# A hybrid encoder block: its 45 inverse square roots move from VectorE to one GpSimd power instruction each

## The chip, the cores and the metric

The kernel runs on one core of a Trainium2 chip. The metric is the device time of one execution in microseconds (us). The engines are named as the profile names them: PE is TensorE (matmuls and transposes), DVE is VectorE, ACT is ScalarE, POOL is GpSimd, SP is SyncE, which issues most DMAs.

## The reference

One encoder block on 1024 tokens of width 1024, all in float32:

```python
h = rmsnorm(x, norm1_w); p = h @ w_in
# branch A: differential attention, 8 heads, with rmsnorm over each head's 128 output channels
# branch B: gated DeltaNet, 8 heads, forward and backward scans
qg, kg = l2norm(qg), l2norm(kg)
og = rmsnorm(o_fwd + o_bwd, gdn_norm_w) * silu(z)
merged = sigmoid(gate_a) * (oa @ w_proj_attn) + sigmoid(gate_g) * (og @ w_proj_gdn)
x = x + merged @ w_out
x = x + expert_choice_ffn(rmsnorm(x, norm2_w), ...)   # 16 experts, 128 tokens each
out = rmsnorm(x, norm_f_w)
def rmsnorm(t, w): return t * lax.rsqrt(mean(t * t) + 1e-6) * w
```

Every `rsqrt` above is what this case is about: one number per token (first norm, router norm, final norm), or per token and head (l2norm of keys and queries, the ends of DeltaNet heads and of attention heads).

## The kernel before

The work is done in stages that overlap: the first norm of 8 tiles of 128 tokens; 8 DeltaNet heads; 8 attention heads; the two branch projections, the output projection and the router; and 16 experts in 64 units. Exact float32 products are made of three fp32r matmuls: each weight is split into a high part (ACT, `cp`) and a low part (a subtraction, on POOL by `ptt` for the dense weights `W`, on DVE for the experts).

**The order is planned.** Every engine call goes through `Emit.op` (line 273) with a planned cost in ns; a greedy list scheduler (`run`, line 356) takes, among all tasks, the operation that can start first by its own clocks of the five engines and a table of latencies between engines (line 52), and writes it into that engine's stream. So the streams are fixed when the program is built, each engine runs its own in order, and a changed cost or a changed engine moves much of what follows, also of what the edit does not name. `e.cp` is ACT's copy, `e.ts`, `e.tt` and `e.stt` are DVE's scalar, two-operand and fused steps, `e.ptt` and `e.pts` are POOL's.

**The root.** `rsqrt` (line 528) computes y = x^(-1/2) on DVE by an integer estimate (two `ts`) and three Newton steps of three instructions, 11 in a chain. `prsqrt` (line 516) does the estimate on DVE and the three Newton steps, of four instructions each, on POOL. The callers are:

- `norm_tile` (line 719): 8 tiles, one column; the result scales the tile on DVE (even tiles) or ACT and POOL (odd ones), then PE transposes it.
- `Head.main` (line 946): 8 heads, 16 columns (keys and queries); `irk`, `rk2`, `bp` and `nbp` follow on DVE.
- `Head.finish` (line 1159): 8 heads, 8 columns; the result times `aq` scales the head's output `oa` on DVE (line 1175, recorded at L409), which PE then transposes.
- `Attn.finish` (line 1368): 8 heads, 8 columns, in the same way.
- `router` (line 1555): `prsqrt` for 7 tiles, `rsqrt` for the last.
- `final_pair` (line 1939): 4 pairs of final row tiles, two columns; and `Experts.last` (line 1877): the last expert's rows.

In the profile, helpers carry the line: L409 is `tt`, L428 and L429 are `ts`, L434 is `stt`, L413 is `ptt`, L403 is `act`, L391 a matmul, L395 a transpose.

Of the kernel before, what the change touches and what calls it, by code (L numbers as in the profile page):

```python
# [108 lines left out]
class Emit:  # L109
# [403 lines left out]
                lambda: (self.nc.gpsimd.tensor_scalar(out, a, s1, None, op0=op0) if s2 is None else  # L513
                         self.nc.gpsimd.tensor_scalar(out, a, s1, s2, op0=op0, op1=op1)), [out], [a], 0, "pts")

    def prsqrt(self, y, x, t):

        i = t[:, 1].bitcast(I32)
        t = t[:, 0]
        self.ts(i, x.bitcast(I32), 1, op0=ALU.arith_shift_right)  # L520
        self.ts(y.bitcast(I32), i, -1.0, float(0x5F3759DF), op0=ALU.mult, op1=ALU.add)
        for _ in range(3):
            self.ptt(t, y, y, ALU.mult)
            self.ptt(t, t, x, ALU.mult)
            self.pts(t, t, -0.5, 1.5)
            self.ptt(y, t, y, ALU.mult)

    def rsqrt(self, y, x, t):

        i = t[:, 1].bitcast(I32)  # L530
        t = t[:, 0]
        self.ts(i, x.bitcast(I32), 1, op0=ALU.arith_shift_right)
        self.ts(y.bitcast(I32), i, -1.0, float(0x5F3759DF), op0=ALU.mult, op1=ALU.add)
        for _ in range(3):
            self.tt(t, y, y, ALU.mult)
            self.stt(t, t, -0.5, x, ALU.mult, ALU.mult)
            self.stt(y, t, 1.5, y, ALU.add, ALU.mult)


class Ctx:  # L540
# [178 lines left out]
def norm_tile(g, st, w1):  # L719
    e = g.e  # L720
    xs = yield from e.new("xs", [P, D])
    e.dma(xs.v, g.ins["x"][st * P:(st + 1) * P, :])
    yield
    ss, rs = g.nsm[:, st:st + 1], g.nsm[:, 8 + st:9 + st]
    e.act(g.jk.v, xs.v, AF.Square, accum_out=ss)
    e.ts(ss, ss, 1.0 / D, 1e-6)
    e.rsqrt(rs, ss, g.nsm[:, 16 + 2 * st:18 + 2 * st].rearrange("p (a b) -> p a b", b=1))
    yield
    if st % 2:
        e.cp(xs.v, xs.v, scale=rs)  # L730
        e.ptt(xs.v, xs.v, w1.v, ALU.mult)
    else:
        e.stt(xs.v, xs.v, rs, w1.v, ALU.mult, ALU.mult)
    pt = yield from e.new("n0", [P, 8, P])
    for d in range(8):
        e.tr(pt[:, d, :], xs[:, d * P:(d + 1) * P], g.ident.v)
    yield
    o = slice(st * P, (st + 1) * P)
    e.cp(g.hh[:, :, o], pt.v)
    e.tt(g.hl[:, :, o], pt.v, f32(g.hh[:, :, o]), ALU.subtract)  # L740
    e.free(xs, pt)

    def done():
        g.tiles.add(st)
        g.hready[0] = g.tiles >= {0, 1, 2, 3}
        g.hready[1] = len(g.tiles) == 8
    e.then(done)
    if st == 7:
        e.free(w1, g.jk)
        e.close("xs", "w1", "n0", "jk")  # L750


def norm_first(g):
    e = g.e
    g.hT = e.now_new("hh", [P, 8, S], F32R), e.now_new("hl", [P, 8, S], F32R)
    g.hh, g.hl = g.hT[0].v, g.hT[1].v
    g.nsm = e.now_new("nsm", [P, 96]).v
    g.hready, g.tiles = [False, False], set()
    w1 = e.now_new("w1", [P, D])
    g.jk = e.now_new("jk", [P, D])  # L760
    e.spawn(norm_tile(g, 0, w1), 0)
    yield
    e.dma(w1.v, bcast(g.ins["norm1_w"], [P, D]))
    e.dma(g.ident.v, g.ins["c_ident"])
    for st in range(1, NT):
        e.spawn(norm_tile(g, st, w1), 0)
        yield
# [96 lines left out]
class Head:  # L864
# [81 lines left out]
    def main(self):  # L946
# [24 lines left out]
                e.free(pt)  # L971
                yield
        e.ts(ss, ss, 1e-6, op0=ALU.add)
        e.rsqrt(rk, ss, rt)
        e.tt(irk, rk[:, 0:8], ss[:, 0:8], ALU.mult)
        e.tt(rk2, rk[:, 0:8], rk[:, 0:8], ALU.mult)
        if not g.logits:
# [181 lines left out]
    def finish(self):  # L1159
# [10 lines left out]
        e.tt(m2, aq, aq, ALU.mult)  # L1170
        e.tt(m2, m2, sq, ALU.mult)
        e.ts(m2, m2, 1.0 / 128, 1e-6)
        e.rsqrt(rr, m2, rt)
        e.tt(rr, rr, aq, ALU.mult)
        e.tt(oa.v, oa.v, bcast(rr[:, :, None], [P, NT, P]), ALU.mult)
        yield
# [48 lines left out]
class Attn:  # L1225
# [142 lines left out]
    def finish(self):  # L1368
        g, e, o, sm = self.g, self.g.e, self.o, self.sm
        ss, rr = sm[:, 0:8], sm[:, 8:16]  # L1370
        e.ts(ss, ss, 1.0 / 128, 1e-6)
        e.rsqrt(rr, ss, sm[:, 16:32].rearrange("p (a b) -> p a b", b=8))
        e.tt(o.v, o.v, bcast(rr[:, :, None], [P, NT, P]), ALU.mult)
        yield
        for half in range(2):
# [179 lines left out]
def router(g, st, xt, po):  # L1555
# [21 lines left out]
        e.free(pt)  # L1577
        yield
    e.ts(ss, ss, 1.0 / D, 1e-6)
    (e.rsqrt if st == NT - 1 else e.prsqrt)(rs, ss, sm[:, 4:6].rearrange("p (a b) -> p a b", b=1))  # L1580
    pl = yield from e.new("gp", [P, 512])
    for d in range(8):
        e.mm(pl[:, 0:16], hT[:, d, :], g.wr[:, d, :], d == 0, d == 7)
# [150 lines left out]
class Experts:  # L1734
# [142 lines left out]
    def last(self, pd):  # L1877

        g, e, x, fs = self.g, self.g.e, self.xl, self.fs
        for c in range(2):  # L1880
            cs = slice(c * 512, c * 512 + 512)
            e.stt(x[:, cs], pd[:, cs], g.hval[:, NE - 1:NE], x[:, cs], ALU.mult, ALU.add)
        ss, rs, rt = fs[:, 64:65], fs[:, 65:66], fs[:, 66:68]
        e.act(pd.v, x.v, AF.Square, accum_out=ss)
        e.ts(ss, ss, 1.0 / D, 1e-6)
        e.rsqrt(rs, ss, rt.rearrange("p (a b) -> p a b", b=1))
        e.stt(x.v, x.v, rs, g.wf.v, ALU.mult, ALU.mult)
        if g.finished < NT:
            yield lambda: g.finished == NT
        e.scatter(g.out, g.tok[:, NE - 1:NE], x.v)  # L1890
# [48 lines left out]
def final_pair(g, st, xs, fs):  # L1939
# [4 lines left out]
        e.act(jk.v, x.v, AF.Square, accum_out=ss[:, i:i + 1])  # L1944
        e.free(jk)
    e.ts(ss, ss, 1.0 / D, 1e-6)
    e.rsqrt(rs, ss, fs[:, 16 + 2 * st:20 + 2 * st].rearrange("p (a b) -> p a b", b=2))
    for i, x in enumerate(xs):
        if i and st < 6:
            e.cp(x.v, x.v, scale=rs[:, 1:2])  # L1950
# [32 lines left out]
def body(tc, ins, out, dbg=None, heads=H):  # L1983
# [3 lines left out]
    with ExitStack() as ctx:  # L1987
# [16 lines left out]
        g.hval = e.now_new("hval", [P, 16])  # L2004
        g.tok = e.now_new("tok", [P, 16], I32)
        g.one = e.now_new("one", [P, 64])
        g.logits = g.gdn_done = g.gdn_close = g.attn_ok = g.routes = g.route0 = g.list1 = g.rank_ok = False
        g.ranked = g.h2_rows = 0
        g.attn_done = g.lanes = g.wo = g.routed = g.scattered = 0
# [148 lines left out]
```

## Time and profile before

| | |
|---|---|
| three runs | 3036.37 to 3043.48 us, median 3042.06 |
| the profiled execution | 3041.05 us |
| its span (first to last instruction) | 3039.3 us |
| granted TensorE clock, mean | 0.981 of full speed |
| PE / DVE / ACT / POOL busy | 95% / 78% / 58% / 19% |
| chain that ended last | PE 70%, DVE 15%, ACT 3%, DMA 3%, POOL 1% |

Read the busy shares first, then the table by stage: a saving on an engine counts only in a stage where some other engine waits for it. The chain that ended last is followed back from the end of the program, at each step to what released it. Times in the rows are us from the start of the span.

### The profile page before, as it was taken

How to read it: one execution, taken by the hardware profiler on the slowest of the kernel's cores; microseconds unless marked ns; L12 is line 12 of the kernel's file. 1: busy time of each engine (PE TensorE's matmuls, PEld its weight loads, DVE VectorE, ACT ScalarE, POOL GpSimd, SP SyncE). 2: the span in 40 equal slices, each digit the busy share in tenths (PEclk: the TensorE clock that was granted, in tenths of full speed). 3: DMA queues.
4: the chain of work that ended last, by engine and by line, in shares of the span. 5: the costliest groups of instructions: out<-in, count | busy, mean ns of one | idle time of the engine just before them, and what ended most of it. 6: DMA issues, size and time to landing. Idle time of an engine off the chain costs nothing.

```text
span 3039.3 us, 40711 instructions
## 1 busy us (share of the span) xinstructions
PE 2874.6 (95%) x14780; PEld 2401.8 (79%) x14780; DVE 2371.7 (78%) x3948; ACT 1752.0 (58%) x2668; POOL 567.5 (19%) x448
## 2 busy tenths in 40 slices
PE   7999999899998999999999997899999999999996
PEld 6787887788787878888888786788888888888884
DVE  7768778777865777777862458899888989989887
ACT  5435445444534666776662323577767777777775
POOL 3222222222212211211216332500000000000001
PEclk9999999999999999999999997899999999999998
DMA  4222322321322111112459736899999999999995
GB/s 139 52 68 83 84 61 60 90 63 52 89 74 61 49 49 49 49 49 56 112 161 290 231 105 246 311 390 378 372 386 381 380 383 377 378 377 381 373 355 235
DMA packets 203642, 598.75 MB, mean 197 GB/s; under 512 B 84384, under 2 KB 102304, under 8 KB 154288
## 3 DMA queue, kind: packets, MB, share of 16 engines
q1 hardware_dynamic: 189856, 562.06, 51.4%
q0 software_dynamic: 13584, 34.08, 4.0%
q8 instruction: 116, 1.90, 0.3%
q14 instruction: 86, 0.70, 0.1%
HBM read 535.19 MB, written 52.49 MB: 193 GB/s over the span
## 4 chain that ended last, share of the span: by engine, by line
PE 70%; DVE 15%; ACT 3%; DMA 3%; issue 3%; SPq 1%; POOL 1%; POOLq 0%; DVEq 0%; ACTq 0%
PE psum L391 66%; DVE B L409 6%; PE psum L395 4%; DVE B L434 4%; ACT B L403 2%; DVE B L451 2%; SPq L483 1%; ACT psum L403 1%; DMA dw<-B 1%; DVE B L428 1%; DVE B L455 0%; POOL W L413 0%; ACT W L403 0%; DMA A<-dh,C 0%; DMA B<-dl 0%
## 5 line engine op out<-in xcount | busy, mean ns | idle before, releaser
L391 PE MATMUL psum<-A,W 128*128 128x512 f32 (+1 forms) x5856 | 1548.6, 404 | 13.8 <-POOL W L413 5.5
L391 PEld LDWEIGHTS psum<-A,W 128*128 128x128 f32 (+1 forms) x5856 | 1068.0, 189 | 213.4 <-DVE A L409 10.2
L391 PE MATMUL psum<-B 128*128 128x128 f32 (+3 forms) x3494 | 651.6, 324 | 15.9 <-DVE B L455 7.6
L391 PEld LDWEIGHTS psum<-B 128*128 128x128 f32 x3494 | 544.8, 191 | 92.4 <-DVE B L455 11.1
L403 ACT ACTIVATE B<-psum 128x512 f32<-128x512 f32 (+4 forms) x612 | 266.4, 441 | 400.4 <-PE psum L395 225.3
L403 ACT ACTIVATE B<-B 128x2048 fp32r<-128x2048 f32 (+4 forms) x341 | 381.8, 1130 | 183.3 <-DVE B L434 80.8
L413 POOL TENSOR_TENSOR W<-W,W 128x1024 fp32r<-128x1024 f32 (+1 forms) x105 | 265.2, 2527 | 945.9 <-ACT W L403 818.1
L409 DVE TENSOR_TENSOR B<-B,B 128x2048 fp32r<-128x2048 f32 (+2 forms) x189 | 377.3, 2006 | 34.0 <-ACT B L403 27.1
L391 PE MATMUL psum<-B,W 128*128 128x512 f32 x1536 | 374.0, 395 | 4.0 <-DVE B L409 3.8
L391 PEld LDWEIGHTS psum<-B,W 128*128 128x128 f32 x1536 | 286.0, 189 | 74.2 <-DVE B L409 14.8
L403 ACT ACTIVATE B<-psum,B 128x128 f32<-128x128 f32 (+2 forms) x264 | 190.9, 728 | 197.4 <-PE psum L391 124.7
L395 PE MATMUL psum<-C,B 128*128 128x128 f32 (+1 forms) x1392 | 218.9, 281 | 71.7 <-DVE B L434 28.3
L409 DVE TENSOR_TENSOR A<-B,A 128x2048 fp32r<-128x2048 f32 x112 | 256.7, 2306 | 15.6 <-ACT A L403 14.5
L391 PE MATMUL psum<-A,B 128*128 128x512 f32 x1024 | 264.5, 398 | 2.3 <-DVE A L409 2.3
L395 PEld LDWEIGHTS psum<-C,B 128*128 128x128 f32 (+1 forms) x1392 | 170.6, 144 | 120.7 <-DVE B L434 35.0
L403 ACT ACTIVATE A<-B 128x2048 fp32r<-128x2048 f32 (+1 forms) x121 | 222.7, 1857 | 41.4 <-PE psum L391 20.6
L391 PE MATMUL psum<-B,B 128*128 128x128 f32 (+1 forms) x1024 | 212.6, 294 | 13.7 <-DVE B L460 11.5
L391 PEld LDWEIGHTS psum<-A,B 128*128 128x128 f32 x1024 | 191.0, 189 | 40.5 <-DVE A L409 3.0
L391 PEld LDWEIGHTS psum<-B,B 128*128 128x128 f32 x1024 | 175.4, 192 | 40.9 <-DVE B L460 14.8
L497 POOL DMA_INDIRECT dx<-B,C x15 | 24.3, 1618 | 953.9 <-ACT B L403 953.9
L451 DVE TENSOR_REDUCE B<-psum 128x1 f32<-128x1024 f32 (+1 forms) x136 | 157.3, 1158 | 53.9 <-PE psum L391 53.0
L413 POOL TENSOR_TENSOR B<-B,B 128x128 f32<-128x128 f32 (+3 forms) x98 | 131.6, 1346 | 308.6 <-ACT B L403 218.8
(116 smaller groups left out, 2852.6 us busy)
## 6 DMA issues: line engine op xcount, KB each, us to landing
B<-in_w_gu_dram SPq DMA_DIRECT2D x154, 1024.0 KB, 7.3
A<-in_w_gu_dram SPq DMA_DIRECT2D x77, 1024.0 KB, 7.3
B<-in_w_dn_dram SPq DMA_DIRECT2D x74, 1024.0 KB, 7.3
A<-in_w_dn_dram SPq DMA_DIRECT2D x40, 1024.0 KB, 7.6
W<-in_w_gu_dram SPq DMA_DIRECT2D x25, 1024.0 KB, 7.1
W<-in_w_gdn_dram SPq DMA_DIRECT2D x32, 512.0 KB, 3.7
B<-dG SPq DMA_DIRECT2D x32, 512.0 KB, 5.6
W<-in_w_proj_dram SPq DMA_DIRECT2D x32, 512.0 KB, 4.6
```

Of the source, the lines that this page charges most:

```text
L391: self.op("pe", c, lambda: self.nc.tensor.matmul(out, lhsT, rhs, start=start, stop=stop), [out], [lhsT, rhs], l, "mm")
L395: self.op("pe", 109, lambda: self.nc.tensor.transpose(out, in_, ident), [out], [in_, ident], 55, "tr")
L403: self.op("act", c, lambda: self.nc.scalar.activation(out, in_, func, **kw), [out] + w, [in_] + r, 0, "act")
L409: self.op("dve", 69 + 1.041 * free(out), lambda: self.nc.vector.tensor_tensor(out, a, b, op), [out], [a, b], 0, "tt")
L413: self.op("pool", 150 + 2.104 * free(out), lambda: self.nc.gpsimd.tensor_tensor(out, a, b, op), [out], [a, b], 0, "ptt")
L428: lambda: (self.nc.vector.tensor_scalar(out, a, s1, None, op0=op0) if s2 is None else self.nc.vector.tensor_scalar(out, a, s1, s2, op0=op0 ...
L434: lambda: self.nc.vector.scalar_tensor_tensor(out, a, s, b, op0=op0, op1=op1),
L451: self.op("dve", 69 + 1.041 * free(in_), lambda: self.nc.vector.tensor_reduce(out, in_, axis=AX.X, op=op), [out], [in_], 0, "red")
L483: self.op("sp", 478, lambda: self.nc.sync.dma_start(out, in_), [out], [in_], 0, "dma", max(n / 360.0, 112))
L497: self.op("pool", 1100, lambda: self.nc.gpsimd.indirect_dma_start(out=dst, out_offset=bass.IndirectOffsetOnAxis(ap=idx, axis=0), in_=y, in ...
```

## The change

`rsqrt` becomes one instruction on POOL: a two-operand instruction with the operation `pow`, whose second operand is a column that holds -0.5, broadcast along the row (`e.half`, column 63 of the tile `one`, set once by a memset on POOL). `prsqrt` and the scratch columns go. The planner is told a cost of 150 + 20 n ns for n columns.

```diff
-    def prsqrt(self, y, x, t):
-
-        i = t[:, 1].bitcast(I32)
-        t = t[:, 0]
-        self.ts(i, x.bitcast(I32), 1, op0=ALU.arith_shift_right)
-        self.ts(y.bitcast(I32), i, -1.0, float(0x5F3759DF), op0=ALU.mult, op1=ALU.add)
-        for _ in range(3):
-            self.ptt(t, y, y, ALU.mult)
-            self.ptt(t, t, x, ALU.mult)
-            self.pts(t, t, -0.5, 1.5)
-            self.ptt(y, t, y, ALU.mult)
-
-    def rsqrt(self, y, x, t):
-
-        i = t[:, 1].bitcast(I32)
-        t = t[:, 0]
-        self.ts(i, x.bitcast(I32), 1, op0=ALU.arith_shift_right)
-        self.ts(y.bitcast(I32), i, -1.0, float(0x5F3759DF), op0=ALU.mult, op1=ALU.add)
-        for _ in range(3):
-            self.tt(t, y, y, ALU.mult)
-            self.stt(t, t, -0.5, x, ALU.mult, ALU.mult)
-            self.stt(y, t, 1.5, y, ALU.add, ALU.mult)
+    def rsqrt(self, y, x):
+
+        n = free(x)
+        h = self.half[:, 0:1] if n == 1 else bcast(self.half[:, 0:1], [P, n])
+        self.op("pool", 150 + 20 * n, lambda: self.nc.gpsimd.tensor_tensor(y, x, h, op=ALU.pow), [y], [x, self.half], 0, "pow")
...
     g.jk = e.now_new("jk", [P, D])
+    e.pset(e.half, -0.5)
...
         e.ts(ss, ss, 1e-6, op0=ALU.add)
-        e.rsqrt(rk, ss, rt)
+        e.rsqrt(rk, ss)
...
         e.ts(m2, m2, 1.0 / 128, 1e-6)
-        e.rsqrt(rr, m2, rt)
+        e.rsqrt(rr, m2)
...
     e.ts(ss, ss, 1.0 / D, 1e-6)
-    (e.rsqrt if st == NT - 1 else e.prsqrt)(rs, ss, sm[:, 4:6].rearrange("p (a b) -> p a b", b=1))
+    e.rsqrt(rs, ss)
...
         g.one = e.now_new("one", [P, 64])
+        e.half = g.one[:, 63:64]
```

The other callers (`norm_tile`, `Attn.finish`, `last`, `final_pair`) lose their scratch argument in the same way.

**How the streams move.** In the program's order a row is line, operation, output<-inputs, size, and how often in a row. L520 is the power instruction; tiles are named by their block (B_80, B_82 and C_76 hold norms, small columns and constants, W_83 and W_108 or W_111 the raw and the split dense weights).

DVE at the start, the first norm, before:

```order
L429 TENSOR_SCALAR C_76<-C_76 128x1
L428 TENSOR_SCALAR C_76<-C_76 128x1
L429 TENSOR_SCALAR C_76<-C_76 128x1
L409 TENSOR_TENSOR C_76<-C_76 128x1
L434 SCALAR_TENSOR_TENSOR C_76<-C_76 128x1 x2
L409 TENSOR_TENSOR C_76<-C_76 128x1
L434 SCALAR_TENSOR_TENSOR C_76<-C_76 128x1
L429 TENSOR_SCALAR C_76<-C_76 128x1
L434 SCALAR_TENSOR_TENSOR C_76<-C_76 128x1
```

and now:

```order
L429 TENSOR_SCALAR C_76<-C_76 128x1
L434 SCALAR_TENSOR_TENSOR B_80<-B_80,C_76 128x1024
L429 TENSOR_SCALAR C_76<-C_76 128x1 x2
L434 SCALAR_TENSOR_TENSOR B_80<-B_80,C_76 128x1024
L409 TENSOR_TENSOR A_79<-psum,A_78 128x8x128
```

The chain of small steps is gone from DVE: the mean plus epsilon (L429) is followed at once by the scaling of the tile (L434, 1024 wide), with the root between them on POOL, where the eight roots stand among the products of the odd tiles:

```order
L420 MEMSET C_76 128x1
L520 ISA
L520 TENSOR_TENSOR C_76<-C_76 128x1 x3
L413 TENSOR_TENSOR B_80<-B_80 128x1024
L520 TENSOR_TENSOR C_76<-C_76 128x1 x2
L413 TENSOR_TENSOR B_80<-B_80 128x1024
L520 TENSOR_TENSOR C_76<-C_76 128x1 x2
L413 TENSOR_TENSOR B_80<-B_80 128x1024
L520 TENSOR_TENSOR C_76<-C_76 128x1
L413 TENSOR_TENSOR W_108<-W_83,W_108 128x256
```

Before, POOL had the products and splits alone there; the last root now stands just ahead of the split of the first weight.

DVE at the end of the last DeltaNet head (8 columns; `oa` is scaled in the last row, B_80 by B_82; the first steps of the root stand just ahead), before:

```order
L409 TENSOR_TENSOR B_7778<-B_82,B_7778 64x1024 x2
L434 SCALAR_TENSOR_TENSOR B_82<-B_82 128x8
L409 TENSOR_TENSOR B_82<-B_82 128x8
L434 SCALAR_TENSOR_TENSOR B_82<-B_82 128x8
L409 TENSOR_TENSOR B_82<-B_82,B_80 128x1024
L409 TENSOR_TENSOR B_80<-B_80 128x1024
L434 SCALAR_TENSOR_TENSOR B_82<-B_82 128x8
L409 TENSOR_TENSOR B_82<-B_82,B_80 128x1024
L409 TENSOR_TENSOR B_82<-B_82 128x8
L434 SCALAR_TENSOR_TENSOR B_82<-B_82 128x8 x2
L409 TENSOR_TENSOR B_82<-B_82 128x8
L409 TENSOR_TENSOR B_80<-B_80,B_82 128x1024
```

and now:

```order
L428 TENSOR_SCALAR B_82<-B_82 128x8
L409 TENSOR_TENSOR B_82<-B_82 128x8 x2
L429 TENSOR_SCALAR B_82<-B_82 128x8
L409 TENSOR_TENSOR B_82<-B_82 128x8
L409 TENSOR_TENSOR B_7528<-B_82,B_7528 64x1024 x2
L409 TENSOR_TENSOR B_80<-B_80,B_82 128x1024
```

Between the sum of squares and the scaling of the head stood five large instructions of the attention's first rotary step; now two do, and the product of the root with `aq` (the second 128x8 row of L409) stands right behind the L429 that feeds the root.

POOL at the same place, the products of qG (B_80 by B_81) and the first key split of the attention (64x1024), before:

```order
L413 TENSOR_TENSOR W_111<-W_83,W_111 128x1024 x3
L413 TENSOR_TENSOR B_80<-B_80,B_81 128x1024 x2
L413 TENSOR_TENSOR W_111<-W_83,W_111 128x1024 x4
L413 TENSOR_TENSOR B_7778<-B_82,B_7778 64x1024 x2
L413 TENSOR_TENSOR W_111<-W_83,W_111 128x1024
```

and now:

```order
L413 TENSOR_TENSOR W_108<-W_83,W_108 128x1024 x2
L413 TENSOR_TENSOR B_80<-B_80,B_81 128x1024 x2
L413 TENSOR_TENSOR W_108<-W_83,W_108 128x1024 x3
L520 TENSOR_TENSOR B_82<-B_82,C_76 128x8
L413 TENSOR_TENSOR W_108<-W_83,W_108 128x1024 x2
L413 TENSOR_TENSOR B_7528<-B_82,B_7528 64x1024 x2
```

The root stands between two runs of weight splits: it can start only when the third split before it is done, and the two behind it start only when its operand has come from DVE.

## Rows read from the trace of the kernel before

**Rows 1.** The page, part 1: busy time (share of the span) and instructions of each engine.

```profile
PE 2874.6 (95%) x14780; PEld 2401.8 (79%) x14780; DVE 2371.7 (78%) x3948; ACT 1752.0 (58%) x2668; POOL 567.5 (19%) x448
```

**Rows 2.** Busy us by stage: from:to, length, PE PEld DVE ACT POOL, clock, DMA, GB/s.

```profile
0.00:45.00 45.00, 25.70 (x170) 22.66 (x171) 27.73 (x111) 25.79 (x37) 14.66 (x10) 0.92 0.48 163
45.00:1000.00 955.00, 893.60 (x5034) 761.59 (x5033) 710.03 (x2012) 423.49 (x1182) 235.93 (x198) 0.99 0.26 70
1000.00:1600.00 600.00, 577.44 (x3331) 492.89 (x3330) 455.01 (x724) 410.83 (x766) 117.08 (x52) 0.99 0.25 73
1600.00:1960.00 360.00, 326.87 (x1510) 268.49 (x1509) 217.69 (x459) 116.42 (x136) 149.56 (x156) 0.93 0.67 230
1960.00:2980.00 1020.00, 1019.58 (x4615) 832.10 (x4614) 916.79 (x563) 748.19 (x518) 40.08 (x28) 1.00 0.98 377
2980.00:3040.00 60.00, 31.42 (x129) 24.10 (x127) 44.39 (x83) 27.32 (x31) 10.15 (x4) 0.79 0.52 211
```

**Rows 3.** Waits of PE from 45 to 1000: waited for, us in total, times, longest.

```profile
PE psum L395 <- DVE B L409: 19.1, 6, 8.8
```

**Rows 4.** Timeline of DVE, 1856.8 to 1861.4: start us, us, engine, line, op, out<-in, shapes.

```profile
1857.08 0.15 DVE L428 TENSOR_SCALAR B<-B 128x1 int32<-128x1 int32 x1
...
1858.62 0.16 DVE L409 TENSOR_TENSOR B<-B 128x1 f32<-128x1 f32 x1
...
1859.20 1.28 DVE L434 SCALAR_TENSOR_TENSOR A<-A,B 128x1024 f32<-128x1024 f32 x1
1861.11 0.17 DVE L451 TENSOR_REDUCE B<-psum 128x1 f32<-128x16 f32 x1 [0.62 <-PE psum L391]
```

**Rows 5.** Groups of DVE by shape, whole span: count | busy us, mean ns | idle before.

```profile
L409 DVE TENSOR_TENSOR B<-B 128x8 f32<-128x8 f32 x88 | 22.3, 258 | 4.2 <-ACT B L403 3.1
...
L434 DVE SCALAR_TENSOR_TENSOR B<-B 128x8 f32<-128x8 f32 x96 | 17.6, 183 | 1.2
...
L434 DVE SCALAR_TENSOR_TENSOR B<-B 128x16 f32<-128x16 f32 x48 | 12.0, 251 | 0.9
```

**Rows 6.** Groups of POOL by shape, whole span.

```profile
L413 POOL TENSOR_TENSOR W<-W,W 128x1024 fp32r<-128x1024 f32 x104 | 264.5, 2544 | 945.9 <-ACT W L403 818.1 <-PE psum L391 86.0 <-PE psum L395 27.3
...
L413 POOL TENSOR_TENSOR B<-B 128x1 f32<-128x1 f32 x63 | 12.0, 191 | 67.3 <-DVE B L429 62.8
```

**Rows 7.** Timeline of POOL, 1842.5 to 1846.2: first and last step of one router root.

```profile
1842.93 0.46 POOL L413 TENSOR_TENSOR B<-B 128x1 f32<-128x1 f32 x2 [8.23 <-DVE B L429]
...
1845.93 0.19 POOL L413 TENSOR_TENSOR B<-B 128x1 f32<-128x1 f32 x1
```

**Rows 8.** Timeline of all engines, 17 to 20.

```profile
15.88 1.14 ACT L403 ACTIVATE B<-B,C 128x1024 f32<-128x1024 f32 x1
...
17.10 2.36 POOL L413 TENSOR_TENSOR B<-B 128x1024 f32<-128x1024 f32 x1 [16.64 <-ACT B L403]
...
17.56 1.92 DVE L434 SCALAR_TENSOR_TENSOR C<-C 128x1 f32<-128x1 f32 x1
```

**Rows 9.** Groups of DVE by shape, 9 to 45.

```profile
L434 DVE SCALAR_TENSOR_TENSOR C<-C 128x1 f32<-128x1 f32 x48 | 10.7, 247 | 0.2
```

**Rows 10.** Timeline of all engines, 43 to 46.

```profile
42.84 1.32 PE L391 MATMUL psum<-A,W 128*32 128x256 f32 x9
...
44.69 1.66 PE L391 MATMUL psum<-A,W 128*128 128x512 f32 x6
```

**Rows 11.** Timeline of all engines, 973.3 to 986: the end of the last DeltaNet head.

```profile
974.07 0.17 DVE L428 TENSOR_SCALAR B<-B 128x8 int32<-128x8 int32 x1
...
980.24 2.30 DVE L434 SCALAR_TENSOR_TENSOR B<-B 128x8 f32<-128x8 f32 x1
...
985.67 0.69 PE L395 MATMUL psum<-C,B 128*128 128x128 f32 x2 [8.79 <-DVE B L409]
```

**Rows 12.** Timeline of all engines, 2993.7 to 3005: the first pair of final rows.

```profile
2993.94 0.17 DVE L428 TENSOR_SCALAR C<-C 128x2 int32<-128x2 int32 x1
...
2996.12 1.29 DVE L434 SCALAR_TENSOR_TENSOR B<-B,C,W 128x1024 f32<-128x1024 f32 x1
```

More of the change, by code (lines that the diff above doesn't have):

```diff
@@ L726, in norm_tile @@
     e.ts(ss, ss, 1.0 / D, 1e-6)
-    e.rsqrt(rs, ss, g.nsm[:, 16 + 2 * st:18 + 2 * st].rearrange("p (a b) -> p a b", b=1))
+    e.rsqrt(rs, ss)
     yield
@@ L1371, in finish @@
         e.ts(ss, ss, 1.0 / 128, 1e-6)
-        e.rsqrt(rr, ss, sm[:, 16:32].rearrange("p (a b) -> p a b", b=8))
+        e.rsqrt(rr, ss)
         e.tt(o.v, o.v, bcast(rr[:, :, None], [P, NT, P]), ALU.mult)
@@ L1579, in router @@
     e.ts(ss, ss, 1.0 / D, 1e-6)
-    (e.rsqrt if st == NT - 1 else e.prsqrt)(rs, ss, sm[:, 4:6].rearrange("p (a b) -> p a b", b=1))
+    e.rsqrt(rs, ss)
     pl = yield from e.new("gp", [P, 512])
@@ L1885, in last @@
         e.ts(ss, ss, 1.0 / D, 1e-6)
-        e.rsqrt(rs, ss, rt.rearrange("p (a b) -> p a b", b=1))
+        e.rsqrt(rs, ss)
         e.stt(x.v, x.v, rs, g.wf.v, ALU.mult, ALU.mult)
@@ L1946, in final_pair @@
     e.ts(ss, ss, 1.0 / D, 1e-6)
-    e.rsqrt(rs, ss, fs[:, 16 + 2 * st:20 + 2 * st].rearrange("p (a b) -> p a b", b=2))
+    e.rsqrt(rs, ss)
     for i, x in enumerate(xs):
```

## The prediction

> **What bounds the kernel now.** I read the page first. Over the whole span TensorE is busy 95%, VectorE 78% and GpSimd 19% [rows 1], so on the average TensorE is the bound and GpSimd has room. An average hides stages, so the next view is the table by stage [rows 2]. In the expert stage (1960 to 2980) TensorE is busy 1019.6 of 1020 us, and no inverse square root stands there: nothing of the change can shorten it. What TensorE leaves idle lies elsewhere: 45.0 − 25.7 = 19.3 us in the first 45 us, 955 − 893.6 = 61.4 in the DeltaNet heads, 600 − 577.4 = 22.6 in the attention, 360 − 326.9 = 33.1 around the router and the top-k, and 28.6 in the last 60 us, part of it after the last matmul. These idle stretches are all that the change can win; VectorE time that is saved while TensorE is busy ends nothing earlier.
>
> The list of waits says who ends TensorE's idle time among the heads [rows 3]: the largest, 19.1 us in 6 waits, is on VectorE's two-operand instruction of line 409 before a transpose, which is the scaling by the root's result at the end of each head. So a share of the idle time hangs on the very chain that is changed.
>
> **The change, part by part.** There are 45 roots: 8 in the first norm (1 column), 8 in the heads' key and query norms (16 columns), 8 at the heads' ends and 8 at the attention heads' ends (8 columns), 8 in the router, 4 for pairs of final rows and 1 last. Of these, 38 lose 11 VectorE instructions each and 7 in the router lose 2 on VectorE and 12 on GpSimd; 45 power instructions come in on GpSimd, and one memset.
>
> *What one root costs before.* With VectorE to itself, the chain runs from 1857.08 to the scaling at 1859.20 [rows 4], 2.1 us, each step about 0.19 us after the one before. In the middle stages the steps are interleaved with others and cost occupancy: 17.6 us for 96 fused steps of 8 columns, 48 of the 88 products of 8 columns at 0.258 (12.4), and 12.0 for 48 fused steps of 16 columns [rows 5]. These three groups are 42 us of the 1165 that VectorE works from 45 to 1600; the products of 16 columns and the integer steps come on top.
>
> *What one power instruction costs.* No row shows it. From below: a product of one column on GpSimd takes 0.191 us, one of 1024 columns 2.544 [rows 6]. From above: GpSimd computed the same function in 12 steps from 1842.93 to 1846.12, 3.2 us [rows 7]. I take a value near the lower end, 0.2 to 0.5 us by width, because it is one instruction of 1 to 16 columns and the two product rows bracket that width; with a hand-over each way (0.08 us from ACT's end at 17.02 to GpSimd's product at 17.10 is the nearest row [rows 8], I take 0.15) a root is back within about 0.8 us, 1.3 less than before. At the upper end it is back after 3.5 us, 1.4 more than before.
>
> *A price beside it.* While GpSimd ran a product of two SBUF operands from 17.10 to 19.46, VectorE's fused step on a single column, begun at 17.56, took 1.92 us in place of about 0.2 [rows 8]: the two hold each other up. The Trainium skill, "GPSIMD Engine Reference", section 1 (Specifications), says that GpSimd shares its SBUF interfaces with VectorE, with contention for instructions of two SBUF inputs; the trace agrees. The power instruction reads two operands too, so it holds VectorE for its own length: 45 × 0.2 to 0.5 us, 9 to 22 us, against the 42 of the middle stages and the 11 of the start that are removed. I leave it out of TensorE's path, as a part of what is saved. The Trainium skill, same page, section 4.1 (Engine selection), rules that elementwise work belongs on VectorE, GpSimd being about twice as slow with two inputs; the rows at one column (0.191 against 0.16 us) do not show that factor, and eleven steps against one outweigh it. By that rule alone, eleven steps doubled, a root would take 4.2 us and the sum would come to the slower rival below.
>
> *Start.* The norm's 8 roots cost VectorE 10.7 us in their fused steps alone [rows 9], while TensorE waits for the normalized tiles; the first large matmul starts at 44.69 [rows 10]. VectorE was busy 27.7 us of these 45 and ACT 25.8 [rows 2]. Without the roots VectorE falls to some 15, so ACT ends last: up to the last tile's scaling it has about 22 of its 25.8 us, which from 9 on end near 31. Behind that come a GpSimd product (2.4 [rows 8]), 8 transposes and the two evictions of a tile (1 to 2 each, taken as 4 in all) and a quarter of the logit matmuls (24 at 1.32/9 = 0.147, 3.5 [rows 10]), near 41. That is −4. Bounds: −8 if GpSimd's last product is not behind the weight splits, +1 if each root takes the upper end. The Trainium skill, same page, section 2.1 (Instruction dispatch), gives about 6 us to the first call of freshly loaded GpSimd code; no row here shows such a gap, and by it the start would give back 2 and the sum would be −14.
>
> *Heads' ends.* Five of the six waits are short (together 19.1 − 8.8 = 10.3); the planner moves the transposes up with the result, so I take back only 3. The sixth is the last head's end: the chain begins at 974.07, loses 2.3 us to a GpSimd product at 980.24 and large instructions between its steps, and TensorE stands 8.79 us until 985.67 [rows 11]. In the new order two large subtractions stand between the sum of squares and the scaling, in place of five large instructions; three of about 1.2 us and the 2.3 fall out of the chain. I take −5. Bounds for both: −17 and +3.
>
> *The rest of heads and attention.* The 42 us of occupancy and more leave stages in which TensorE is busy 94 to 96%. About a tenth of them reaches TensorE, whose idle share there is 84 of 1555 us, 5%, and which waits for VectorE in the largest of the listed waits: −5. Bounds: −15 and +15, the latter the wait of the new in-order hop, below.
>
> *Router.* The last tile's root is ready at 1859.2, and the step that uses it waits for TensorE until 1861.11 [rows 4]: 0. In the others 12 GpSimd steps become one, off TensorE's path: 0, bounds −3 and +1.
>
> *Tail.* In the final pairs the chain stands alone on VectorE, 2993.94 to 2996.12, ahead of the steps that the last matmuls wait for [rows 12]. Two roots before the last matmuls give 1.3 each and the last pair some 0.5: −3. Bounds −5 and 0.
>
> **Sum.** −4 − 3 − 5 − 5 + 0 − 3 = −20 us against the profiled execution's 3041.05, its span of 3039.3 included: 3021. The median of the three runs shown is 1.0 higher, so the forecast is **3022 us**.
>
> **Rivals.** *No change (within 9 us, 0.3%, which is about what a measurement of this kernel can tell).* Only start and tail stay, −7: 3035. For it: TensorE is at 95%, and a new static order has new waits elsewhere as the old one had. Against: the named waits stand on the chain itself.
>
> *More than forecast.* If the short waits and VectorE's occupancy come back in full, start −8, ends −15, rest −15, tail −4: 3000. For it: DVE ends most of TensorE's waits. Against: TensorE can win no more than its idle share.
>
> *Slower: the root waits in GpSimd's queue.* Before, the chain depended on nobody. Now the power instruction stands in order behind splits of weights, 2.54 us each, which themselves wait for ACT (818.1 us of idle time before 104 of them) [rows 6], and VectorE, in order, waits for its result with everything behind it. If at the 16 roots of the heads it comes a split later than planned, TensorE loses 16 × 2.54 = 41 us; less start and tail, +34: 3075. It decides from the point where a root comes back later than the old 2.1 us. For it: GpSimd is busy 25% from 45 to 1000 (235.9 of 955 us [rows 2]), and its rows of waits are long. Against: the planner gives the queue its place, and splits are made a job ahead. An upper-end power instruction (3.2 us) ends here too. The Trainium skill's rule on elementwise work (section 4.1, above) speaks for this rival.
>
> *The change does nothing of the kind*: were the instruction expanded into many by the compiler, the order would show it; it shows one row each. No chance of its own.
>
> **How the numbers follow.** Forecast 0.52 (3008 to 3033), more than forecast 0.14, no change 0.20, slower 0.14. Faster by over 0.3% (under 3033) is the first two, 0.66. The range reaches from 3000, the rival of more, to 3045, which holds most of no change and leaves out the slower rival: 3000 to 3045.
>
> **What would show it.** Right: power instructions of 0.2 to 0.5 us; the first large matmul near 41; no wait near 8.8 us before the last head's transposes; VectorE's busy time some 50 to 80 us lower; an expert stage of the same length that begins some 15 to 18 us earlier. Wrong: power instructions of microseconds; VectorE's waits for GpSimd among its largest; TensorE's waits for VectorE in the heads as long as before; longer waits for the weight splits.

## The result and the profile after

The changed kernel takes **3069.48 us** (median of 4 runs, 3063.45 to 3070.47) against 3042.06 of the kernel before on the same chip: a ratio of 1.0089, 95% interval [1.0074, 1.0104]. It is slower by 27 us. The forecast was 3022, its range 3000 to 3045; only the slower rival (3075) names the right side.

The profiled execution took 3069.17 us, its span 3067.4. The page's first part, busy times and counts by engine (compare [rows 1]):

```profile
PE 2887.8 (94%) x14780; PEld 2402.3 (78%) x14780; DVE 2308.3 (75%) x3516; ACT 1749.3 (57%) x2668; POOL 615.9 (20%) x410
```

VectorE is relieved of 432 instructions and 63 us, as forecast (50 to 80). The kernel is slower all the same. The groups of GpSimd by shape show what the new instruction (line 520) costs (count | busy us, mean ns | idle us before, and what ended it):

```profile
L520 POOL TENSOR_TENSOR B<-B,C 128x8 f32<-128x8 f32 x16 | 26.8, 1676 | 146.9 <-DVE B L429 139.8 <-DMA dgate<-W 7.0
L520 POOL TENSOR_TENSOR B<-B,C 128x16 f32<-128x16 f32 x8 | 24.2, 3022 | 94.5 <-DVE B L428 94.5
...
L520 POOL TENSOR_TENSOR B<-B,C 128x1 f32<-128x1 f32 x8 | 4.4, 554 | 89.3 <-DVE B L429 89.3
...
L520 POOL TENSOR_TENSOR C<-C,C 128x2 f32<-128x2 f32 x4 | 2.8, 703 | 36.5 <-DVE C L429 36.4
```

One column takes 0.55 us, two 0.70, eight 1.68, sixteen 3.02 in the mean: some 0.16 us for each further column. The forecast had 0.2 to 0.5. The plan that orders the program was told 150 + 20 ns a column, so 0.31 us at 8 columns and 0.47 at 16. The idle time before these groups ends almost wholly with VectorE, not with a split of weights: GpSimd stands ready and waits for the operand.

The table by stage, cut where TensorE has about as many matmuls behind it as in [rows 2] (from:to, length, PE, PEld, DVE, ACT, POOL, granted clock, DMA, GB/s):

```profile
0.00:45.00 45.00, 25.37 (x171) 23.00 (x172) 15.94 (x23) 25.73 (x37) 18.24 (x19) 0.92 0.48 162
45.00:1020.70 975.70, 905.75 (x5049) 765.76 (x5048) 684.37 (x1835) 423.09 (x1183) 274.18 (x214) 0.98 0.25 69
1020.70:1628.90 608.20, 577.79 (x3314) 490.52 (x3314) 445.75 (x637) 408.72 (x765) 131.25 (x60) 0.99 0.24 72
1628.90:1993.60 364.70, 328.14 (x1514) 267.31 (x1513) 211.88 (x435) 117.34 (x137) 138.93 (x81) 0.93 0.66 228
1993.60:3014.00 1020.40, 1019.45 (x4613) 831.53 (x4612) 916.48 (x561) 747.37 (x518) 40.39 (x28) 1.00 0.98 377
3014.00:3067.40 53.40, 31.25 (x128) 24.21 (x126) 33.88 (x28) 27.02 (x31) 12.89 (x9) 0.81 0.58 235
```

Against the lengths in [rows 2] the start gains nothing, the DeltaNet heads lose 20.7 us, the attention 8.2, the stretch around the router 4.7, the expert stage 0.4, and the tail (59.3 us to the end of the span before) gains 5.9: together +28.1, the difference of the spans. The loss lies where the 24 roots of 8 and 16 columns are. There VectorE has a wait that did not exist before (its list of waits; waited for, us in total, times, longest):

```profile
DVE B L409 <- POOL B L520: 36.2, 20, 3.0
DVE C L409 <- POOL B L520: 6.4, 4, 1.8
```

These are 24 waits, one for each of the 24 large roots, and 42.6 us together.

One of them, the key and query root of a head, on VectorE's, GpSimd's and TensorE's timelines (start, us, engine, line, op, out<-in, shapes, the idle time before and its releaser):

```profile
413.92 0.17 DVE L428 TENSOR_SCALAR B<-B 128x16 f32<-128x16 f32 x1 [1.42 <-ACT psum L403]
414.19 0.29 DVE L455 COPY B<-psum 128x128 f32<-128x128 f32 x1
417.11 0.24 DVE L409 TENSOR_TENSOR B<-B 128x8 f32<-128x8 f32 x2 [2.63 <-POOL B L520]
417.27 0.28 DVE L455 COPY B<-psum 128x128 f32<-128x128 f32 x1
```

```profile
414.18 2.90 POOL L520 TENSOR_TENSOR B<-B,C 128x16 f32<-128x16 f32 x1 [14.41 <-DVE B L428]
```

```profile
415.04 0.71 PE L391 MATMUL psum<-A,W 128*128 128x512 f32 x2
417.61 0.49 PE L391 MATMUL psum<-B 128*128 128x128 f32 x2 [1.85 <-DVE B L455]
417.85 0.71 PE L391 MATMUL psum<-A,W 128*128 128x512 f32 x2
418.40 0.61 PE L391 MATMUL psum<-B,B 128*128 128x128 f32 x4
418.84 2.26 PE L391 MATMUL psum<-B 128*128 128x256 f32 x6
```

The plan put one copy between the root's operand (413.92) and its first user. The root comes back after 3 us, VectorE stands 2.63 us at the user, the copy queued behind it comes late, and TensorE waits 1.85 us for that copy, which has nothing to do with the root.

### The profile page after: what moved, and what is told of

Its sections match the earlier page's. It is cut to its first block, busy times and chain, and to the rows that moved or that the text cites. A ratio compares the mean times of both kernels' runs of the same rounds, so it can differ in the third digit from the quotient of the medians.

```text
span 3067.4 us, 40226 instructions
## 1 busy us (share of the span) xinstructions
PE 2887.8 (94%) x14780; PEld 2402.3 (78%) x14780; DVE 2308.3 (75%) x3516; ACT 1749.3 (57%) x2668; POOL 615.9 (20%) x410
## 5 line engine op out<-in xcount | busy, mean ns | idle before, releaser
L409 DVE TENSOR_TENSOR B<-B,B 128x2048 fp32r<-128x2048 f32 (+2 forms) x189 | 372.3, 1981 | 44.1 <-ACT B L403 25.7
L409 DVE TENSOR_TENSOR A<-B,A 128x2048 fp32r<-128x2048 f32 x112 | 256.7, 2307 | 14.6 <-ACT A L403 14.6
```

The source lines that it names most:

```text
L409: self.op("dve", 69 + 1.041 * free(out), lambda: self.nc.vector.tensor_tensor(out, a, b, op), [out], [a, b], 0, "tt")
```

## The experiments

Three theories. **The price**: the plan was told a false duration and left no room behind a root. **The order**: the new plan is worse by itself, whatever a root takes. **The latency**: a root on another engine costs its 0.55 to 2.9 us in any order. Each experiment was timed beside the kernel before, whose median there lay between 3037.82 and 3040.30 us; the ratios are to it.

"Root" says what is issued for a root: the power instruction, the old chain of steps, or a product by 0.0005, which leaves the inverse square root out and only takes its place. "A nanosecond off" is a plan with one unrelated cost changed by 1 ns.

| run | plan | root | us | ratio to before [95%] |
|---|---|---|---|---|
| the change | told 150 + 20n | power | 3069.48 | 1.0089 [1.0074, 1.0104] |
| e1 | same | product | 3029.51 | 0.9964 [0.995, 0.9978] |
| e7 | same | product at 8, 16 columns | 3031.56 | 0.9973 [0.9958, 0.9989] |
| e8 | same | old chain | 3116.25 | 1.0252 [1.0231, 1.0273] |
| e2 | that of before | power | 3013.67 | 0.9914 [0.9897, 0.993] |
| e5 | that of before | product | 3013.54 | 0.9916 [0.9894, 0.9937] |
| e3 | told 400 + 156n | power | 3044.79 | 1.0015 [1.0004, 1.0026] |
| e6 | told 400 + 156n | product | 3037.50 | 0.9989 [0.9978, 1.0] |
| e4 | before, a nanosecond off | old chain | 3047.76 | 1.003 [1.0021, 1.004] |
| e9 | 150 + 20n, a nanosecond off | power | 3077.88 | 1.0136 [1.0119, 1.0153] |
| e10 | e4's | power | 3025.94 | 0.9955 [0.9938, 0.9972] |
| e11 | 400 + 156n, a nanosecond off | power | 3055.20 | 1.0055 [1.0039, 1.0072] |
| e12 | told 800 + 312n | power | 3090.13 | 1.0176 [1.0159, 1.0193] |
| e13 | told 2000 | power | 3046.12 | 1.0011 [1.0001, 1.002] |
| e14 | 400 + 156n, and the chain's VectorE steps | power | 3039.15 | 0.9997 [0.9988, 1.0007] |
| e15 | large roots as before | power | 3019.03 | 0.9925 [0.9909, 0.9942] |
| e16 | 400 + 156n, not counted on GpSimd | power | 3036.58 | 0.9987 [0.9976, 0.9997] |

### The root's duration taken away, the order kept (e1, e7)

The edit, abridged:

```diff
-    self.op("pool", 150 + 20 * n, lambda: ...tensor_tensor(y, x, h, op=ALU.pow), ...)
+    self.op("pool", 150 + 20 * n, lambda: ...tensor_tensor(y, x, h, op=ALU.mult), ...)
-    e.pset(e.half, -0.5)
+    e.pset(e.half, 0.0005)
```

(e7: the product only where n is 8 or more; its 0.0005 stands in a column of its own, and the small roots keep the power.)

> The changed kernel with the same instructions in the same order on every engine, except that each of the 45 power instructions is a product of the same operands (the column holds 0.0005 instead of -0.5). No inverse square root is computed here: each root is replaced by x times 0.0005. Theory 1 (the price): the power instruction takes 0.55 to 2.90 us where the planner was told 0.17 to 0.47, and VectorE, which runs in order, stands at the root's first user. The product should take about 0.2 us for one column and under 0.5 us for 16, so that the time falls to 3020 to 3045 us, the three heads' groups of rows gain their 1.4 to 2.6 us each, and VectorE's wait for GpSimd (36.2 us in 20 pieces in the changed kernel) falls below 10 us. Theory 2 (the order): the new plan is a worse order by itself, whatever a root takes. Then the time stays at 3060 to 3075 us with the waits of TensorE for VectorE where they were.

> The changed kernel in its own order, where only the 24 roots of 8 and 16 columns (heads and attention) are products by 0.0005, so that no inverse square root is computed there; the 21 roots of one and two columns (start, router, tail) stay power instructions. Theory 1 by the rows' own durations (16 x 1.65 + 8 x 2.90 us against 17 x 0.55 + 4 x 0.70): nearly all of the 40 us lies in the large roots, so 3029 to 3036 us. If it were the handing over between the engines, which each of the 45 pays alike, rather than the duration, about half would come back: 3045 to 3055.

The order is the same row for row, and 40 us are gone (3069.48 to 3029.51). With the small roots left as powers it is 38 (3031.56): what a shorter root gives back lies in the 24 large ones, so it goes by duration, not by handing over, which all 45 pay alike. GpSimd's groups and VectorE's wait in e1:

```profile
L520 POOL TENSOR_TENSOR B<-B,C 128x8 f32<-128x8 f32 x16 | 4.1, 254 | 147.0 <-DVE B L429 131.4 <-DMA dgate<-W 15.5
L520 POOL TENSOR_TENSOR B<-B,C 128x16 f32<-128x16 f32 x8 | 2.7, 338 | 94.1 <-DVE B L428 94.1
```

```profile
DVE B L409 <- POOL B L520: 1.7, 5, 0.4
```

At the place shown above, TensorE's timeline in e1 has no hole, and the same six matmuls take 1.25 us in place of 2.26:

```profile
402.56 0.71 PE L391 MATMUL psum<-A,W 128*128 128x512 f32 x2
403.11 0.38 PE L391 MATMUL psum<-B 128*128 128x128 f32 x2
403.24 0.70 PE L391 MATMUL psum<-A,W 128*128 128x512 f32 x2
403.79 0.61 PE L391 MATMUL psum<-B,B 128*128 128x128 f32 x4
404.23 1.25 PE L391 MATMUL psum<-B 128*128 128x256 f32 x6
```

### The old order, with the power instruction (e2, e5)

The edit, abridged and in part in words (a router root keeps its fourteen steps in the plan):

```diff
 def rsqrt(self, y, x, t):
-    self.ts(i, ...); self.ts(y, ...); three times self.tt, self.stt, self.stt
+    the same eleven steps counted with their costs, none of them issued;
+    at the first: self.nc.gpsimd.tensor_tensor(y, x, h, op=ALU.pow)
```

(e5: the product by 0.0005 in its place.)

> The kernel before with its plan untouched: the planner still counts the eleven (or fourteen) steps of each root, but none of them is issued, and one power instruction on GpSimd is issued where the first of them stood. Every other instruction stands on its engine in the order of the kernel before. Theory 1 (the price): the chain's place in the plan is 1 to 3 us wide, and other work of VectorE stands between its steps, so that a power instruction of 0.55 to 2.90 us fits into most of it: 3020 to 3045 us, not over the kernel before. Theory 2 (the new order): the same, 3020 to 3045, since the order is the old one. Theory 3 (the latency itself costs, in whichever order: VectorE to GpSimd and back, and 1.7 to 2.9 us at 8 and 16 columns against the chain's 2.1 us): 3055 to 3080 us, with VectorE's waits for GpSimd at 30 us or more.

> The kernel of the run before with the old plan (3013.67 us), with a product by 0.0005 in place of each power instruction; no inverse square root is computed here. It asks what the power instruction's own time still costs in the old order. In the new order that was 40 us (3069.48 against 3029.51). Theory 1 (the new plan left no room behind a root, the old one does): 2 to 15 us here, so 2999 to 3012 us. Theory 3 (the root's time costs the same in any order): 30 to 45 us, 2970 to 2985. Theory 2 (order alone, no price): no difference, 3011 to 3016.

With every other instruction where it stood before, the same 45 power instructions make the kernel **faster by 26 us** (ratio 0.9914), though they take about as long as after the change. That is below the 3020 to 3045 that two theories gave. A product in their place gains nothing more (3013.54; the price theory expected 2 to 15 us here, the order theory none): the old order hides them, as far as these runs can tell. GpSimd's groups, VectorE's largest wait for a root, and the timelines at the root that matches the one above:

```profile
L520 POOL TENSOR_TENSOR B<-B,C 128x8 f32<-128x8 f32 x16 | 27.5, 1716 | 140.2 <-DVE B L429 113.9 <-DVE B L409 22.1 <-DVE B L428 4.1
L520 POOL TENSOR_TENSOR B<-B,C 128x16 f32<-128x16 f32 x8 | 26.0, 3256 | 79.9 <-DVE B L428 63.5 <-PE psum L391 16.4
```

```profile
DVE B L409 <- POOL B L520: 3.0, 3, 1.7
```

```profile
387.93 0.16 DVE L428 TENSOR_SCALAR B<-B 128x16 f32<-128x16 f32 x1
388.00 1.28 DVE L434 SCALAR_TENSOR_TENSOR B<-B,C,B 128x1024 f32<-128x1024 f32 x1
389.20 0.88 DVE L460 STREAM_TRANSPOSE B<-B 128x128 f32<-128x128 f32 x4
390.01 0.40 DVE L463 COPY_PREDICATED B<-C,psum 128x256 f32<-128x256 uint32 x1
```

```profile
388.24 3.80 POOL L520 TENSOR_TENSOR B<-B,C 128x16 f32<-128x16 f32 x1 [5.13 <-DVE B L428]
```

The old chain had other work planned between its steps. Without the steps that work is what VectorE does while GpSimd computes the root. The theory of the latency, which expected 3055 to 3080 us here, falls.

### The order alone (e8)

The edit, abridged:

```diff
-    self.ts(i, ...); self.ts(y, ...); three times self.tt, self.stt, self.stt
+    self.op("pool", 150 + 20 * n, go, [y], [x, self.half], 0, "pow")   # go issues those steps
```

> The changed kernel's plan on every engine, with the old eleven VectorE steps (at the router's seven the old two and twelve) issued in the place of each power instruction: the order alone is changed against the kernel before. Theory 1 (the plan left 0.17 to 0.47 us for a root, and the chain takes 2.1 us or more, on VectorE itself): 3060 to 3085 us, no better than with the power instruction, since VectorE carries the 63 us again. Theory 2 (the order is worse for itself by some 15 us, as 3029.51 against 3013.67 us hints): 3050 to 3060. An order that is no worse: 3035 to 3045.

3116.25 is above every theory's range. In the new order the old chain costs 76 us more than in its own (3039.98 beside it); there its steps stand in one block on VectorE, with one copy and then its first user behind them (first and last step, copy, user):

```profile
428.08 0.17 DVE L543 TENSOR_SCALAR B<-B 128x16 int32<-128x16 int32 x1
...
430.17 0.17 DVE L548 SCALAR_TENSOR_TENSOR B<-B 128x16 f32<-128x16 f32 x1
430.26 0.28 DVE L455 COPY B<-psum 128x128 f32<-128x128 f32 x1
430.46 0.23 DVE L409 TENSOR_TENSOR B<-B 128x8 f32<-128x8 f32 x2
```

In that same order the power instruction is 47 us better than the chain. So the change's instruction is a gain in either order, 26 us in the old and 47 in the new, and its plan is a loss under either root, 76 us under the chain and 56 under the power (3069.48 against 3013.67). One less the other is the change's loss, 29 or 30 us by these runs; what the instruction is worth depends on the order that it stands in. Of the plan's loss 16 us stay even with a product (e1 against e5): that part is the theory of the order.

### The true price, and a plan that means nothing (e3, e6, e4, e9 to e11)

```diff
-    self.op("pool", 150 + 20 * n, ...)
+    self.op("pool", 400 + 156 * n, ...)          # e3; with the product, e6
-    self.op("dve", 69 + 1.041 * free(out), ... tensor_tensor ...)
+    self.op("dve", 68 + 1.041 * free(out), ... tensor_tensor ...)   # e4, e9, e10, e11
```

> The changed kernel with one number of the plan changed: the planner counts a power instruction at 400 + 156 ns for each column, as the trace measures it, instead of 150 + 20. Theory 1 in its form that the false cost is at fault: the planner puts other work between root and user, and the time falls to 3025 to 3045 us, VectorE's wait for GpSimd to under 15 us. Theory 3 (the latency costs even where it is planned for): 3055 to 3075 us. Theory 2 (each new plan lands somewhere): anything from 3030 to 3090, and the waits of VectorE for GpSimd say nothing on it.

> The plan with the measured price (400 + 156 ns a column), with a product by 0.0005 in place of each power instruction; no inverse square root is computed here. With the power instruction this plan took 3044.79 us, 31 us more than the old order with it. If the plan, told the truth, hides the instruction, the product gains 0 to 10 us (3035 to 3045), and the 31 us are the order's alone. If it hides it no better than the false plan, the product gains 25 to 40 us (3005 to 3020).

> The kernel before, with the roots as they were, and one cost of the plan changed by a nanosecond (VectorE's tensor_tensor counted at 68 instead of 69 ns plus its columns). The order changes (some 750 of TensorE's rows stand elsewhere), no instruction does. How far do plans scatter that mean nothing? Theories 1 and 3 (the root's own time makes the 27 us): the time stays within 8 us of the kernel before, 3034 to 3050. Theory 2 (the order): shifts of 15 us and more, either way, come from such a re-plan alone.

> The changed kernel with one unrelated cost of its plan changed by a nanosecond (VectorE's tensor_tensor at 68 instead of 69 ns plus its columns; some 900 of TensorE's rows stand elsewhere). If the loss is the price that the plan was told, any plan made with it loses: 3055 to 3085 us, with VectorE's waits for GpSimd at 30 us or more. If the changed kernel's order was an unlucky draw: 3030 to 3050.

> The plan of the fourth run (the kernel before with VectorE's tensor_tensor at 68 ns, 3047.76 us with the old chains), kept row for row, with the power instruction where each chain's first step stood. If the 26 us that the power instruction gained in the old order are VectorE's removed work, whatever the draw, they come here too: 3018 to 3028 us. If the old order was a lucky draw for it: 3035 to 3055.

> The plan with the measured price (400 + 156 ns a column), and the same unrelated nanosecond (VectorE's tensor_tensor at 68). It tells how far plans with the true price scatter. If 3044.79 us is what such a plan gives, 3037 to 3053; if it was an unlucky draw, down to 3015 to 3030.

One number of the plan gives back 25 us (3044.79, still 5.5 above the kernel before beside it), and VectorE's wait for the large roots falls:

```profile
DVE B L409 <- POOL B L520: 9.5, 7, 2.0
```

A product gains 7 us more there (e6), against 40 under the false price. Each of these two contrasts lies within one order, so no accident of ordering enters them: what a root's duration costs falls from 40 to 7 us once the plan is told of it. The nanosecond moves the times by 8 to 12 us, all four upwards (e4, e9, e11, and e10, which has e4's plan), so differences of about 10 between two plans are read as nothing; this rests on one such tweak. The contrasts outlast it: against e4 the false price loses 30 us (e9), the true price 7 (e11, 2 us above its forecast of 3037 to 3053), and the power instruction in e4's own order gains 22 (e10). The false price is the cause of most of what the change lost. It is not why the true price wins nothing: both its plans stay above the kernel before.

### Why the true price does not reach the old order (e12 to e16)

The plan was changed alone: twice the price (e12), a flat 2000 ns (e13), the true price with the chain's VectorE steps counted beside it and awaited by nobody (e14), the old chain counted for the 24 large roots only (e15), the true price on an engine that exists only in the plan (e16).

> The changed kernel with the power instruction counted at twice its measured price (800 + 312 ns a column: 3.3 us at 8 columns, 5.8 at 16). If room behind the root is all that matters, this plan hides it as the old order does, and the product's 7 us of the true price come back: 3030 to 3040 us. If the plan's clock suffers from a false price in either direction: 3045 to 3065. If the plan with the chains was good for the 2 to 3 us that it held VectorE busy there, and no price on GpSimd stands in for that: 3037 to 3050.

> The changed kernel with every power instruction counted at 2000 ns, whatever its columns: about the width that the old chain had in the plan (some 2.2 us with the handing over between its steps), without its hold on VectorE. If the width behind the root is what the old plan had to give: 3015 to 3030 us. If it was VectorE's reserved time: 3040 to 3060. If a price that is too high on GpSimd does harm of its own, as twice the true price did (3090.13 us): 3050 to 3090.

> The power instruction planned on GpSimd at its measured price, and the chain's eleven VectorE steps still counted beside it without being issued, so that VectorE has 0.8 to 1.0 us of slack at each root but nobody waits for these steps. If VectorE's reserved time is what the old plan had to give: 3015 to 3030 us. If not: 3035 to 3055, as the true price alone (3044.79).

> The 24 roots of 8 and 16 columns planned as the old chains (counted, not issued, the power instruction at the first step's place), and those of one and two columns at the power instruction's measured price, except the router's seven, which keep their old plan. If the old plan's advantage lies in the large roots of the heads and the attention: 3015 to 3030 us. If it lies in the small ones at the start or in the draw: 3035 to 3055.

> The measured price (400 + 156 ns a column), but in the plan the power instruction holds an engine of its own, so that the plan neither makes it wait for GpSimd's weight splits nor holds GpSimd for it; on the chip it is issued on GpSimd as ever. The old chain's plan had this in common: no root was counted on GpSimd there, except the router's. If the counting on GpSimd is what keeps the true price 30 us above the old plan: 3015 to 3028 us. If not: 3035 to 3055, as with the true price on GpSimd (3044.79).

More room is not better: at twice the price VectorE waits for the large roots 5.1 us in all, yet the time is 3090.13, the worst with a power instruction and above every forecast for it, and TensorE's waits in e12 have moved to other lines and to ACT (top of its list):

```profile
PE psum L395 <- DVE B L434: 21.2, 16, 4.3
PE psum L395 <- ACT B L403: 19.8, 5, 13.3
PE psum L391 <- ACT B L403: 18.8, 15, 6.2
```

The chain's width alone (e13), its hold on VectorE alone (e14) and leaving GpSimd out of the count (e16) all stay within 10 us of each other, 3036.58 to 3046.12, no further apart than a nanosecond moves a plan, and within 6 us of the kernel before. Only the chain itself, counted for the large roots, comes near the old order's time with the power instruction (3019.03 against 3013.67). What in it does so, beyond these three parts, stays open; each of the five is a single plan. For use the answer is there: e2, at 3013.67 us, beats both kernels (the changed one by 56 us).

## Why the prediction was wrong

**The price of the power instruction** is the step that failed. The text took "a value near the lower end, 0.2 to 0.5 us by width", because product rows bracketed the width. That the nearest rows were of another operation was the flaw: 0.55, 0.70, 1.68 and 3.02 us were measured, at 16 columns nearly the upper bound of 3.2. The 191 ns do hold for what they showed: in e1 a product of 8 columns takes 254 ns. So e1 also tells what the rest of the sum was worth: its products of 0.19 to 0.34 us are the price that the forecast assumed, in the change's own order, and it takes 3029.51 us, 10 below the kernel before beside it and inside the range, though half of the gain of 20 that was forecast. Of the 47 us between forecast and result, 40 are the price and some 7 the other terms.

**The point from which a slow root decides** was put at "later than the old 2.1 us". At 8 columns the root is back in 1.8 us, sooner than the chain, and VectorE still stood up to 1.8 us at its user: in an order written down beforehand what counts is when the plan expects it. "The planner moves the transposes up with the result" was right, and was the harm: it moved them to where the result would have been at 0.31 us. The diff shows 150 + 20 n; the forecast shared that error instead of doubting it.

**The price beside it**, power instructions that hold VectorE for their own length, did not show: VectorE is busy 2308.3 us with them and 2311.8 with products in the same order (e1). It went the other way where the two met. In e2, above, VectorE's large instruction from 388.00 took 1.28 us, and the power instruction beside it 3.80 where most of 16 columns take 2.90.

**Start**, −4: measured 0. TensorE's first large matmul stands at 44.61 (44.69 in [rows 10]). VectorE did fall to 15.94 us. But from 26 on TensorE was itself the bound before, busy all 19 us at a granted clock of 0.86, which the forecast did not read:

```profile
26.00:45.00 19.00, 19.00 (x143) 17.04 (x142) 11.27 (x29) 9.26 (x13) 7.93 (x3) 0.86 0.25 67
```

After the change it was busy 17.76 us of the same stretch at 0.82, so the earlier operands won nothing. In e2 the stretch runs at 1.00, and the matmul comes at 42.26 (the change, then e2):

```profile
26.00:45.00 19.00, 17.76 (x131) 16.43 (x132) 5.14 (x7) 8.05 (x14) 7.95 (x5) 0.82 0.24 67
```

```profile
26.00:45.00 19.00, 19.00 (x145) 16.85 (x145) 8.47 (x8) 8.64 (x14) 8.50 (x4) 1.00 0.18 57
```

**Heads' ends and the rest of heads and attention**, −13 together: measured +20.7 and +8.2 in their stages. The named wait of 8.79 us before the last head's transposes [rows 11] did shrink, to 3.92 (at 1002.86), and VectorE's occupancy did fall; the 24 waits for GpSimd took more than that back. The bounds of these two terms (+3, +15) were too narrow, as they priced an upper-end root by its hop alone and not by the work queued behind its user.

**Router**, 0: +4.7 in a stretch that begins right behind the last attention root (1618.86); which wait in it makes them was not tried. **Tail**, −3: −5.9. The pair's root, alone on VectorE before from 2993.94 to 2996.12 [rows 12], is shorter here, 0.85 us from the end of its operand to the scaling:

```profile
3027.45 0.16 DVE L429 TENSOR_SCALAR C<-C 128x2 f32<-128x2 f32 x1
3027.70 0.72 POOL L520 TENSOR_TENSOR C<-C,C 128x2 f32<-128x2 f32 x1 [29.12 <-DVE C L429]
...
3028.46 1.28 DVE L434 SCALAR_TENSOR_TENSOR B<-B,C,W 128x1024 f32<-128x1024 f32 x1 [0.85 <-POOL C L520]
```

**The slower rival** gave 3075, near the result, for a reason that did not hold: the roots hardly queue behind splits of weights, GpSimd waits for VectorE. That its number came so near is luck; its last clause, an upper-end instruction, is what came. The Trainium skill, "GPSIMD Engine Reference", section 4.1 (Engine selection), puts elementwise work on VectorE and not on GpSimd; e8 against the change shows the power instruction 47 us ahead of the chain in one and the same order, so here it is not the engine that lost. The expert stage kept its length, as forecast, and carried the lag through unchanged.

## What to carry to other kernels

Where a program's order is computed from a table of costs, a guess at an instruction that no trace has shown yet goes into the whole order. Measure the instruction first by itself, or put it into the old order, whose other places are known to work; here that was the best of all, and a plan made anew with the measured price did not reach it. A saving on a busy engine is worth only what the work queued behind it can use; look at what is queued behind the first user of a result, and not only at the user. And keep the plan apart from the instruction in the experiment: here the instruction was a gain in every order in which it was set against the chain, and the plan that came with it a loss.

## What was not expected

- The power instruction is priced by the column: 0.55 us for one column, 2.90 (the median) for 16, while a product is nearly flat there (0.19 to 0.34 us).
- The handing over is short: 0.09 us from VectorE's end to GpSimd's start (3027.61 to 3027.70) and 0.04 back (3028.42 to 3028.46). The Trainium skill, "GPSIMD Engine Reference", section 2.1 (Instruction dispatch), gives about 6 us to the first call of freshly loaded code. No run here shows it: the first power instruction took 0.57 us at 9.54, after 8.71 us in which GpSimd had waited for VectorE, so that such a load could also have passed unseen.
- A wait of TensorE can cost twice. After the 1.85 us above, its granted clock stood at 1.00 until 418.80 and at 0.52 from 418.80 to 422.20, near the lower of its two levels, 1.2 and 2.4 GHz; in e1, without the wait, the same matmuls ran at 1.00 (windows of the change, then of e1):

```profile
418.80:422.20 3.40, 3.40 (x15) 3.03 (x15) 1.59 (x7) 0.90 (x3) 0.45 (x1) 0.52 0.00 0
```

```profile
404.20:406.20 2.00, 2.00 (x15) 1.88 (x14) 1.34 (x6) 0.92 (x4) 0.46 (x1) 1.00 0.00 0
```

Over the span TensorE is busy 2887.8 us after the change and 2876.2 in e1, in the same order with the same instructions: 11.6 of the 40 us are matmuls that took longer, the rest is standing still. The old order shows it too: in e2 TensorE is busy 2866.3 us against 2874.6 before, so 8 of the 28 us by which its span is shorter (3011.3 against 3039.3) are not idle time won. The prediction had taken the idle time for all that the change can win.
